# Recurrent mixer of a hybrid encoder: level products of both directions in one group, projection banks emptied by ScalarE ahead of the sigmoids, outputs in the places of the level tiles

## The chip, the core and the metric

The kernel runs on one core of one Trainium2 chip. Its engines have names in the profile: PE is TensorE (PEld its weight loads), DVE VectorE, ACT ScalarE, POOL GpSimd, SP SyncE, which issues most of the DMAs. The metric is the device time of one execution in microseconds (us), as the median of several runs; one further execution is taken by the profiler, and all busy times, waits and windows come from that one.

## What is computed

The program is a two-layer encoder trunk on 1024 tokens of width 1024 in fp32. Layer 0 mixes tokens by windowed attention, layer 1 by a bidirectional gated linear recurrence (HGRN2); in both, four more heads attend to 256 memory tokens (the cross heads), and a ConvGLU channel mixer follows. Only layer 1's recurrence is touched. It has 8 heads of 128 keys and 128 values. Cut to what matters:

```python
q, i, zf, zb, gate, xq = split(u @ w_in, ...)        # 8 heads x 128 each, xq for the cross heads
q = silu(q); v = i
f = lb + (1 - lb) * sigmoid(z)                        # z = zf forward, zb backward
log_f, k = log(f), 1 - f
# per direction, over time:  S_t = diag(f_t) S_(t-1) + k_t v_t^T ;  o_t = q_t S_t
o = gla(q, k_f, v, log_f_f) + flip(gla(flip(q), flip(k_b), flip(v), flip(log_f_b)))
o = rmsnorm(o, norm_g) * silu(gate)                   # per head
y = concat([o, cross_attention(xq, mem_kv)]) @ w_out
```

## The kernel before

Every fp32 product against a weight is done as three products of rounded halves: `mm3` (L79 to L82) writes high by high, high by low, low by high into one PSUM bank. A weight unit of 128 x 1024 is loaded, rounded by ACT (L75) and its remainder taken by DVE (L76). The normed input of the layer stands transposed in SBUF as `uh`, `ul`.

**Layer 1's mixer** is `hgrn()`. Per head `proj(h)` makes the projections: `proj_fm` the query `q` and the two forget inputs `s` (f and b), each in two halves of 512 tokens with channels on partitions, and `proj_tm` the value `V` and gate `G` for two heads at once with tokens on partitions. All of them fill banks with the tag `pj`, of which there are two. Forget banks are emptied by one Exp on ACT. Query and gate banks go through `sigmoid` (L1100 to L1102: Exp, Ln, Exp on ACT, written to SBUF) and then a DVE product that reads the bank once more (L1124, L1138), so a bank is held until that product. `ORD` is a table of text that sets the order of loads and projections per head; projections of head h+1 are written in the program behind head h. Odd heads have six banks to project (q, f, b in two halves), even heads besides these the values and gates of two heads. The last head's row leaves two of its projections ("later") between its directions.

**A head** (`head`) calls `direction` four times, in the order (forward, first half), (backward, second half), (forward, second half), (backward, first half); I call them A, B, C, D, or first to fourth. A direction goes over 512 tokens in four chunks of 128:

- ACT makes log f (`Ln` at L1188, tile `a_`) and k (L1186, L1187, L1189); DVE scans (L1191) within blocks of 16; ACT takes exponentials `EP`, `ER` (L1198, L1199) and two more (L1211, L1212).
- DVE and POOL form the operands of three levels (blocks of 16, 32 and 64, L1213 to L1235). A step of each level multiplies the decays of neighbouring blocks together. The operand tiles are `E1`, `E2`, `G32` and `G`.
- PE forms the level products into the bank `pa` of the direction (`block`, L1217 to L1219), each on a strip of 32 columns of the array (`tile_position`): 8 products of 64 columns, 16 of 32 for the blocks of 16, 8 of 32 for the next level.
- DVE picks the valid entries into `Az` (L1258), ACT or POOL adds the directions into `As` (L1262, L1264).
- PE transposes `ER` (L1267) into a bank `pt`, ACT copies it to `kT` (L1270), PE multiplies by v into `pu` (L1273), and DVE updates the states `S` (L1280).

Then `output` runs for the second and the first half: PE sums `As` by v and the decayed queries by `S` into `po` (L1295), ACT takes squares (L99), POOL the power (L92), DVE scales (`on`, L1302), PE transposes (L1306), ACT writes `ot` (L1325) and SP stores it. For the last head `ot` isn't stored; it becomes operand of the output projection. Between directions and outputs, `cross` puts units of the cross heads (`cross_unit`, L198 to L240), as `HX` says: in even heads one after C and one after D. A unit ends with ACT's copy to `xo` (L238) and its DMA. In the stretch of the last head the output projection's first pass (bank `pb`) starts.

**What sets the order.** The engines' instruction order is fixed when the program is built. A planner takes the program as written, runs a time model of its own, and lets instructions of later parts go ahead where their tiles are to be had; `high_priority(AHEAD)` lets a few go first, `issue_after` holds some behind another. A tile with a tag takes one of a fixed number of places, and these are handed out in the order in which the program asks for them: a tile gets its place when the tile that held it has had its last reader. On each engine the instructions then run strictly in the built order. Before, the tag `E` has 5 places and a direction asks for 7 of them (`a_`, `R`, `B`, `E1`, `E2`, `G32`, `G`); `q` has 3 places, `s` 5; `ot` and `xo` share one place of their own; `kT`, `on`, and the pairs for x and p one each.

Of the kernel before, what the change touches and what calls it, by code (L numbers as in the profile page):

```python
# [8 lines left out]
F32 = mybir.dt.float32  # L9
# [9 lines left out]
P = 128  # L19
# [27 lines left out]
def build(tc, A, out):  # L47
# [149 lines left out]
    def cross_unit(l, h, b, head, wp, tags, w0, pair, dead=False):  # L197
# [39 lines left out]
        ot = p[:, :2, :].rearrange("p a b -> p (a b)") if dead else w0.tile([P, 512], F32, tag=tags.get("xo", "xo"), bufs=1, name="xo")  # L237
# [802 lines left out]
    def hgrn():  # L1040
# [18 lines left out]
        tags = {"pj": ("pj", 2, psj), "ps": ("pt", 2, Bank), "pt": ("pt", 2, Bank), "po": [lambda x=x: bank(x, (P, 512)) for x in ("po", "pu")], "sm": 1, "xo": "ot"}  # L1059
# [11 lines left out]
        for d in range(2):  # L1071
            gf = early.tile([P, 512], F32, tag="E", bufs=5, name="gf")
            nc.sync.dma_start(gf, A["gmask"][d])
            dve.tensor_copy(gm[d], gf)
# [23 lines left out]
        def sigmoid(o, z):  # L1098

            act.activation(o, z, AF.Exp, scale=-1.0)  # L1100
            act.activation(o, o, AF.Ln, bias=1.0)
            act.activation(o, o, AF.Exp, scale=-1.0)  # L1102

        def proj_tm(h, us, ts):
# [3 lines left out]
            for t in ts[::2]:  # L1108
# [10 lines left out]
                for x in range(2):  # L1119
                    g = G[:, two, t + x, :]  # L1120
                    with tc.high_priority(AHEAD):
                        dve.tensor_copy(V[:, two, t + x, :], ps[x][:, :, 0, :])
                        sigmoid(g, ps[x][:, :, 1, :])
                        dve.tensor_tensor(g, ps[x][:, :, 1, :], g, op=ALU.mult)  # L1124

        def proj_fm(h, r, us, bws):
            for b, w in bws:
# [6 lines left out]
                if w == 0:  # L1134
                    q = eq.tile([P, 512], F32, tag="q", bufs=3, name="q")
                    with tc.high_priority(AHEAD):
                        sigmoid(q, ps)
                        dve.tensor_tensor(q, ps, q, op=ALU.mult)  # L1138
# [32 lines left out]
        def direction(h, r, d, b, qin, S, As):  # L1171
# [5 lines left out]
            def E():  # L1177
                return early.tile([P, 512], F32, tag="E", bufs=5, name="E")
# [9 lines left out]
            act.activation(a_, k, AF.Ln, bias=lb[:, d, h:h + 1], scale=oml[:, d, h:h + 1])  # L1188
            act.activation(k, k, AF.Identity, bias=oml[:, d, h:h + 1], scale=noml[:, d, h:h + 1])  # L1189
            R, B = E(), E()  # L1190
            dve.tensor_tensor_scan(B[:, rev], smask, a_[:, rev], 0.0, op0=ALU.mult, op1=ALU.add)  # L1191
# [8 lines left out]
            pa = PA[d]  # L1200
            E1, E2 = E(), E()
            Bl, Be = halves(B, 16)
            Rl, Re = halves(R, 16)
# [7 lines left out]
            act.activation(e1, Re, AF.Exp, scale=-1.0)  # L1211
            act.activation(l2, Bl, AF.Exp, scale=-1.0)  # L1212
# [4 lines left out]
            def block(c, i, j, x, y, n=32):  # L1217

                return pe.matmul(pa[i:i + 32, c, j:j + n], x[:, c * P + i:c * P + i + 32], y[:, c * P + j:c * P + j + n],  # L1219
                                 start=True, stop=True, tile_position=(0, i))  # L1220

# [36 lines left out]
            dve.copy_predicated(Az[d], gm[d], pa.rearrange("p c t -> p (c t)"))  # L1258
            a2 = lambda x: x.rearrange("p c t -> p (c t)")
# [322 lines left out]
```

## Time and profile before

| | |
|---|---|
| median of 3 runs | 2642.74 us (2639.37 to 2643.58) |
| the profiled execution | 2641.9 us, span 2640.1 us |
| mean granted TensorE clock | 0.997 |
| busy in the span | PE 98%, DVE 67%, ACT 53%, POOL 18% |
| recurrent mixer, 1212 to 1890 us | PE 667.86 of 678 us, DVE 478.83, ACT 381.11, POOL 175.52, granted clock 1.00, DMA share 0.32 |

Rows of the profile read so: a group has its line, engine, operation and tiles (out<-in), the count behind x, then busy us and mean ns of one, then the idle time of the engine just before and what ended it. A row of the timeline begins with start and duration in us. A matmul's recorded duration includes its way through the array: back to back, products of 512 columns start closer together than their durations say. A wait row names engine, tile and line that waited, what released it, and total us, times, longest us.

### The profile page before, as it was taken

What the parts mean: (1) busy time and instruction counts of PE and PEld (TensorE: products, weight loads), DVE (VectorE), ACT (ScalarE), POOL (GpSimd) and SP (SyncE); (2) the same over time, 40 slices, a digit from 0 to 9 for tenths busy, and PEclk for the clock granted to TensorE, in tenths of its full rate; (3) what the DMA queues carried; (4) which work ended last, traced back from release to release, by engine and by line L of the source; (5) the groups of instructions that cost most, each with busy time, mean ns of one, the idle gap of its engine ahead of it and who ended that gap; (6) DMA issues with size and microseconds to landing.
All of it is one profiled execution on the core that took longest, in us unless ns stands there. A gap on an engine that the chain in (4) does not pass through costs nothing.

```text
span 2640.1 us, 38891 instructions
## 1 busy us (share of the span) xinstructions
PE 2595.8 (98%) x14372; PEld 2180.1 (83%) x14372; DVE 1757.6 (67%) x2852; ACT 1400.3 (53%) x2534; POOL 470.5 (18%) x520
## 2 busy tenths in 40 slices
PE   8999999999999999999999999999999999999998
PEld 8988888888888888887888878888887788888887
DVE  6778777587565565487577685767657665656457
ACT  6667767445444445455465564646434444444443
POOL 0421110221111100032134131221211111110013
PEclk9999999999999999999999999999999999999999
DMA  9782232467877756773236351113337777775666
GB/s 356 248 190 47 74 114 61 131 185 187 215 195 202 196 160 222 220 265 123 84 114 158 94 119 41 61 48 97 120 112 198 197 193 199 205 203 168 201 210 235
DMA packets 195727, 425.92 MB, mean 161 GB/s; under 512 B 20049, under 2 KB 56273, under 8 KB 189905
## 3 DMA queue, kind: packets, MB, share of 16 engines
q1 hardware_dynamic: 161552, 324.06, 37.9%
q0 software_dynamic: 24544, 90.19, 16.3%
q10 hardware_dynamic: 9440, 9.19, 1.0%
q8 instruction: 113, 1.85, 0.3%
q14 instruction: 78, 0.63, 0.1%
HBM read 330.04 MB, written 116.39 MB: 169 GB/s over the span
## 4 chain that ended last, share of the span: by engine, by line
PE 83%; DVE 8%; DMA 4%; ACT 3%; issue 1%; POOL 1%; SPq 0%; ACTq 0%; DVEq 0%; POOLq 0%
PE X L584 28%; PE V L584 10%; PE pj L80 7%; PE pj L81 7%; PE pj L82 7%; PE Y L584 5%; PE pb L80 4%; PE pb L81 4%; PE pb L82 4%; PE po L1295 1%; PE pt L386 1%; PE pa L1219 1%; PE pu L1273 1%; DVE wl L86 1%; PE po L390 1%
## 5 line engine op out<-in xcount | busy, mean ns | idle before, releaser
L86 DVE TENSOR_TENSOR wl<-st,wh 128x1024 fp32r<-128x1024 f32 (+1 forms) x238 | 263.3, 1112 | 314.0 <-ACT wh L85 283.1
L85 ACT CAST wh<-st 128x1024 fp32r<-128x1024 f32 (+1 forms) x238 | 222.5, 936 | 278.3 <-PE X L584 173.8
L584 PE MATMUL X<-wl,wh 128*128 128x512 f32 x528 | 205.0, 390 | 0.2 <-DVE wl L86 0.2
L80 PE MATMUL pj<-uh,wh 128*128 128x512 f32 x512 | 203.5, 398 | 1.7 <-DVE q L1138 1.4
L584 PE MATMUL X<-wh,wl 128*128 128x512 f32 x528 | 204.9, 389 | 0.0
L81 PE MATMUL pj<-ul,wh 128*128 128x512 f32 x512 | 202.3, 395 | 0.0
L82 PE MATMUL pj<-uh,wl 128*128 128x512 f32 x512 | 201.8, 394 | 0.0
L584 PE MATMUL X<-wh 128*128 128x512 f32 x528 | 198.8, 390 | 0.1
L80 PE MATMUL pj<-wh,uh 128*128 128x384 f32 (+1 forms) x512 | 188.3, 369 | 2.1 <-DVE gs L1124 1.2
L81 PE MATMUL pj<-wl,uh 128*128 128x384 f32 (+1 forms) x512 | 187.1, 365 | 0.0
L82 PE MATMUL pj<-wh,ul 128*128 128x384 f32 (+1 forms) x512 | 187.0, 365 | 0.0
L584 PE MATMUL V<-uh,wl 128*128 128x512 f32 x336 | 130.7, 389 | 0.0
L584 PE MATMUL V<-ul,wh 128*128 128x512 f32 x336 | 130.7, 389 | 0.0
L584 PE MATMUL V<-uh,wh 128*128 128x512 f32 x336 | 130.7, 389 | 0.0
L76 DVE TENSOR_TENSOR wl<-st,wh 128x1024 fp32r<-128x1024 f32 (+1 forms) x90 | 114.3, 1274 | 24.3 <-ACT wh L75 22.6
L584 PEld LDWEIGHTS X<-wl,wh 128*128 128x128 f32 x528 | 99.1, 188 | 21.5 <-DVE wl L86 0.9
L584 PEld LDWEIGHTS X<-wh 128*128 128x128 f32 x528 | 99.0, 188 | 21.3 <-ACT wh L85 0.6
L584 PEld LDWEIGHTS X<-wh,wl 128*128 128x128 f32 x528 | 99.1, 188 | 20.6
L80 PEld LDWEIGHTS pj<-uh,wh 128*128 128x128 f32 x512 | 96.2, 188 | 20.5 <-DVE q L1138 2.0
L75 ACT CAST wh<-st 128x1024 fp32r<-128x1024 f32 (+1 forms) x96 | 96.6, 1013 | 29.9 <-PE pj L81 15.4
L82 PEld LDWEIGHTS pj<-uh,wl 128*128 128x128 f32 x512 | 96.3, 188 | 18.9
L81 PEld LDWEIGHTS pj<-ul,wh 128*128 128x128 f32 x512 | 96.4, 188 | 18.4 <-DVE ul L86 0.4
(410 smaller groups left out, 7117.7 us busy)
## 6 DMA issues: line engine op xcount, KB each, us to landing
st<-hid SPq DMA_DIRECT2D x154, 256.0 KB, 3.2
st<-in_ffw_dram SPq DMA_DIRECT2D x108, 256.0 KB, 3.3
w2s<-in_ffw_dram POOLq DMA_DIRECT2D x24, 1024.0 KB, 8.4
st<-in_ffw_dram SPq DMA_DIRECT2D x46, 512.0 KB, 4.5
hid<-tt SPq DMA_DIRECT2D x88, 256.0 KB, 4.7
st<-w2s SPq DMA_DIRECT2D x88, 256.0 KB, 3.1
sx<-in_ffw_dram SPq DMA_DIRECT2D x84, 256.0 KB, 3.9
sy<-in_ffw_dram SPq DMA_DIRECT2D x42, 512.0 KB, 6.2
```

What stands on the lines that cost most here:

```text
L75: act.copy(h[:, :n], raw)
L76: (eng or dve).tensor_tensor(l[:, :n], raw, h[:, :n].bitcast(F32), op=ALU.subtract)
L80: pe.matmul(o, ah, bh, start=first, stop=False)
L81: pe.matmul(o, ah, bl, start=False, stop=False)
L82: return pe.matmul(o, al, bh, start=False, stop=last)
L85: act.copy(h, src)
L86: dve.tensor_tensor(l, src, h.bitcast(F32), op=ALU.subtract)
L386: pe.transpose(tp[:, j, :], sm[:, j, c * P:(c + 1) * P], ident)
L390: pe.matmul(po, v[:, lo + c, :], pl, start=False, stop=c == hi - lo - 1)
L584: last = pe.matmul(o, x, y, start=first and i == 0, stop=i == len(ops) - 1, skip_group_check=not first)
L1219: return pe.matmul(pa[i:i + 32, c, j:j + n], x[:, c * P + i:c * P + i + 32], y[:, c * P + j:c * P + j + n], start=True, stop=True, tile_po ...
L1273: pe.matmul(pu[:, c, :], kT[:, c, :], r["v"][:, 4 * b + c, :], start=True, stop=True)
```

## The change

Three edits, all in `hgrn()` and in the line of `cross_unit` that places its output.

1. **Level products.** `direction` no longer issues them; it returns its operand tiles. A new function `scores` issues them for both directions after each pair (A, B) and (C, D): first the products of 64 columns, each held behind the last and the two directions taking turns (they use different pairs of strips), then the blocks of 16 of both, then those of 32. `Az` and `As` follow there. A direction now uses `E1` and `E2` in place of `a_`, `R` and `B`, so it asks for 4 places of E and not 7.
2. **Projection banks.** Query and gate banks are emptied by ACT: an Exp into a tile `e` (one place) and a copy of the raw values to SBUF. Ln, Exp and the DVE product then work in SBUF; for the gate both token halves of 256 are merged into 512.
3. **Places.** Ring E has 8 places instead of 5, and `xo` and `ot` now draw from it. `kT` shares the place of `on`; the cross pairs for x and p share one pair of places.

```diff
-        ot = ... w0.tile([P, 512], F32, tag=tags.get("xo", "xo"), bufs=1, name="xo")
+        ot = ... w0.tile([P, 512], F32, tag=tags.get("xo", ("xo", 1))[0], bufs=tags.get("xo", ("xo", 1))[1], name="xo")
...
-        tags = {..., "xo": "ot"}
+        tags = {..., "xo": ("E", 8)}
...
-        def sigmoid(o, z):
+        def sigmoid(o):
 
-            act.activation(o, z, AF.Exp, scale=-1.0)
             act.activation(o, o, AF.Ln, bias=1.0)
             act.activation(o, o, AF.Exp, scale=-1.0)
+
+        def etile():
+            return wp.tile([P, 512], F32, tag="e", bufs=1, name="e")
...
-                for x in range(2):
-                    g = G[:, two, t + x, :]
-                    with tc.high_priority(AHEAD):
+                e = etile()
+                e4 = e.rearrange("p (h x c) -> p h x c", h=2, x=2)
+                g = G[:, two, t:t + 2, :]
+                with tc.high_priority(AHEAD):
+                    for x in range(2):
+                        act.activation(e4[:, :, x, :], ps[x][:, :, 1, :], AF.Exp, scale=-1.0)
                         dve.tensor_copy(V[:, two, t + x, :], ps[x][:, :, 0, :])
-                        sigmoid(g, ps[x][:, :, 1, :])
-                        dve.tensor_tensor(g, ps[x][:, :, 1, :], g, op=ALU.mult)
+                        act.copy(G[:, two, t + x, :], ps[x][:, :, 1, :])
+                    sigmoid(e)
+                    dve.tensor_tensor(g, g, e4, op=ALU.mult)
...
+                    e = etile()
                     with tc.high_priority(AHEAD):
-                        sigmoid(q, ps)
-                        dve.tensor_tensor(q, ps, q, op=ALU.mult)
+                        act.activation(e, ps, AF.Exp, scale=-1.0)
+                        act.copy(q, ps)
+                        sigmoid(e)
+                        dve.tensor_tensor(q, q, e, op=ALU.mult)
...
-                return early.tile([P, 512], F32, tag="E", bufs=5, name="E")
+                return early.tile([P, 512], F32, tag="E", bufs=8, name="E")
...
-            a_ = E()
+            E1, E2 = E(), E()
...
-            R, B = E(), E()
+            R, B = E1, E2
...
-            act.activation(e1, Re, AF.Exp, scale=-1.0)
-            act.activation(l2, Bl, AF.Exp, scale=-1.0)
+            act.activation(e1, e1, AF.Exp, scale=-1.0)
+            act.activation(l2, l2, AF.Exp, scale=-1.0)
...
-            with tc.high_priority(AHEAD):
-                for c in range(4):
-                    for o in (0, 32):
-                        mm = block(c, er * 64 + o, lt * 64, G, G, 64)
-                with tc.issue_after(mm.ins):
-                    for c in range(4):
-                        for o in range(0, P, 32):
-                            block(c, o, o, E2, E1)
-                    for c in range(4):
-                        for o in (0, 64):
-                            block(c, o + er * 32, o + lt * 32, G32, G32)
...
-            kT = wp.tile([P, 4, P], F32, tag="kT", bufs=1, name="kT")
+            kT = wp.tile([P, 4, P], F32, tag="on", bufs=1, name="kT")
...
+            return E1, E2, G32, G
+
+        def scores(ops, bs, As):
+
+            def block(d, c, i, j, x, y, n=32):
+                return pe.matmul(PA[d][i:i + 32, c, j:j + n], x[:, c * P + i:c * P + i + 32], y[:, c * P + j:c * P + j + n],
+                                 start=True, stop=True, tile_position=(0, i))
+
+            with tc.high_priority(AHEAD):
+                mm = None
+                for c in range(4):
+                    for d in (1, 0):
+                        G = ops[d][3]
+                        for o in (0, 32):
+                            with tc.issue_after(mm.ins) if mm else nullcontext():
+                                mm = block(d, c, d * 64 + o, (1 - d) * 64, G, G, 64)
+                with tc.issue_after(mm.ins):
+                    for d in (1, 0):
+                        for c in range(4):
+                            for o in (0, 32, 64, 96):
+                                block(d, c, o, o, ops[d][1], ops[d][0])
+                    for c in range(4):
+                        for d in (1, 0):
+                            for o in (0, 64):
+                                block(d, c, o + d * 32, o + (1 - d) * 32, ops[d][2], ops[d][2])
+            a2 = lambda x: x.rearrange("p c t -> p (c t)")
+            for d in (0, 1):
+                b = bs[d]
+                dve.copy_predicated(Az[d], gm[d], a2(PA[d]))
...
-            ot = wp.tile([P, 512], F32, tag="ot", bufs=1, name="ot").rearrange("p (c t) -> p c t", c=4)
+            ot = early.tile([P, 512], F32, tag="E", bufs=8, name="ot").rearrange("p (c t) -> p c t", c=4)
...
-                return [wp.tile([P, 512], F32R, tag=kind + c, bufs=1, name=kind + c) for c in "hl"]
+                return [wp.tile([P, 512], F32R, tag="x" + c, bufs=1, name=kind + c) for c in "hl"]
...
-                direction(h, r, d, b, qin[d], S[d], As)
+                ops[d] = direction(h, r, d, b, qin[d], S[d])
+                if i % 2:
+                    scores(ops, (b, 1 - b) if d == 0 else (1 - b, b), As)
```

Lines behind these edits have other numbers in the changed kernel: the Ln of log f is L1197 there, the ER transposes L1249, the state products L1255, the level products L1269, `Az` L1292, the output products L1311, the `on` transposes L1322 and `ot` L1341.

How the built order moves shows at three places. The first is ACT between heads 4 and 5 before the change: head 5's first direction (L1186 to L1212) amid cross work of head 4 (`ph`), ahead of head 4's `ot`, which comes further down.

```order
L85 CAST ph<-pt 128x512
L1143 ACTIVATE s<-pj 128x512
L1186 ACTIVATE s<-s 128x512
L1187 ACTIVATE s<-s 128x512
L1188 ACTIVATE E<-s,lb,oml 128x512
L1189 ACTIVATE s<-s,oml,noml 128x512
L85 CAST ph<-pt 128x512
L1270 COPY kT<-pt 128x384
L1198 ACTIVATE EP<-E 128x512
```

The same place of ACT after the change, with `xo`, both `ot` of head 4, and then head 5's Ln:

```order
L238 COPY xo<-pu 128x512
L1341 ACTIVATE ot<-pt,bng 128x512
L99 ACTIVATE junk,oss<-po 128x128
L239 DMA oT_58<-xo 128x512
L193 CAST kvh<-kvl 128x512
L1341 ACTIVATE ot<-pt,bng 128x512
L1197 ACTIVATE E<-s,lb,oml 128x512
L1198 ACTIVATE s<-s,oml,noml 128x512
L1207 ACTIVATE EP<-E 128x512
L1208 ACTIVATE ER<-E 128x512
```

Head 5's Ln has moved from ahead of head 4's last `ot` to right behind it; the same holds for every head from 1 to 7.

The second place is PE at the same point after the change: the end of head 4's last output (`po`), a cross unit's last products (`pu<-ph,kvh`), the transposes of `on`, and head 5's first ER transposes.

```order
L1311 MATMUL po<-S,qin 128x128 x2
L80 MATMUL pu<-ph,kvh 128x512
L81 MATMUL pu<-pl,kvh 128x512
L82 MATMUL pu<-ph,kvl 128x512
L1322 MATMUL pt<-ident,on 128x128 x4
L1249 MATMUL pt<-ident,ER 128x128 x4
L80 MATMUL pj<-uh,wh 128x512
L81 MATMUL pj<-ul,wh 128x512
```

Before, head 5's first ER transposes (L1267) stood amid projection products; now nothing stands between them and the transposes of `on`. In front of head 3 it is the same, in front of head 1 there are 38 products between, in front of head 7 there are 11, and in front of heads 2, 4 and 6 there are 63 to 76.

The third place is PE in the last head after the change, from the last `pb` product of the output projection ahead of it (11 such stand behind head 6's `on` transposes) to its last direction.

```order
L82 MATMUL pb<-wh,ul 128x512
L1249 MATMUL pt<-ident,ER 128x128 x4
L1255 MATMUL pu<-v,kT 128x128 x4
L1269 MATMUL pa<-E 32x64 x16
L1269 MATMUL pa<-E 32x32 x48
L1249 MATMUL pt<-ident,ER 128x128 x4
L1255 MATMUL pu<-v,kT 128x128 x4
L1249 MATMUL pt<-ident,ER 128x128 x3
L1255 MATMUL pu<-v,kT 128x128 x3
L1269 MATMUL pa<-E 32x64 x16
L1269 MATMUL pa<-E 32x32 x48
L1249 MATMUL pt<-ident,ER 128x128 x3
```

Before, the four directions of head 7 had `pb` products between them; now the four follow one another, and the `pb` products stand ahead of them and behind the outputs.

More of the change, by code (lines that the diff above doesn't have):

```diff
@@ L1169, in proj, with direction @@
             return r
-        def direction(h, r, d, b, qin, S, As):
+        def direction(h, r, d, b, qin, S):
             q, k = r["q"][b], r["s"][d][b]
@@ L1339, in cross @@
                     xhead[0] = cross_head(1, xh_, wp)
-                cross_unit(1, xh_, xb_, xhead[0], wp, tags, wp, pair, not units)
+                cross_unit(1, xh_, xb_, xhead[0], wp, tags, early, pair, not units)
         def head(h, r):
```

31 lines of the change are left out of this document (11 added, 20 removed).

## The prediction

> **What bounds the kernel now.** I read the page's busy shares first, then the stretch table for the mixer's eight heads, then TensorE's waits in it.
>
> ```profile
> PE 2595.8 (98%) x14372; PEld 2180.1 (83%) x14372; DVE 1757.6 (67%) x2852; ACT 1400.3 (53%) x2534; POOL 470.5 (18%) x520
> 1237.00:1868.00 631.00, 622.53 (x5022) 523.27 (x5020) 445.83 (x885) 352.04 (x756) 166.13 (x178) 1.00 0.31 89
> PE pt L1267 <- ACT ot L1325: 2.6, 2, 1.4
> PE pt L1306 <- DVE on L1302: 2.1, 3, 1.2
> PE pu L1273 <- DVE S L1280: 1.8, 2, 1.4
> PE pj L80 <- DVE q L1138: 1.4, 1, 1.4
> PE pj L80 <- DVE gs L1124: 1.2, 1, 1.2
> ```
>
> The second row runs from the first to the last group of level products: 631.00 us, then busy time of PE, PEld, DVE, ACT, POOL, the granted clock, DMA. PE works 622.5 of 631 at full clock; ACT's 352 and DVE's 446 are cover. The waits (total, times, longest) are all the mixer loses. So only PE counts: a change pays in PE's work or those few waits, and costs where it makes PE wait. PE keeps its order, so what stands ahead of a waiting instruction is all that hides the wait.
>
> **Level products: -16.** One direction's group in before:
>
> ```profile
> 1237.43 0.39 PE L80 MATMUL pj<-uh,wh 128*128 128x512 f32 x1
> 1237.66 0.39 PE L81 MATMUL pj<-ul,wh 128*128 128x512 f32 x1
> 1237.98 1.17 PE L1219 MATMUL pa<-E 128*32 128x64 f32 x64
> 1239.08 0.50 PE L82 MATMUL pj<-uh,wl 128*128 128x512 f32 x1
> 1239.41 0.39 PE L80 MATMUL pj<-wh,uh 128*128 128x512 f32 x1
> ...
> L1219 PE MATMUL pa<-E 128*32 128x32 f32 x1536 | 27.2, 199 | 0.0
> ```
>
> From L81's start to the last row's are 1.75 us with two 512-column products, whose starts are 0.23 apart (first two rows): the group costs 1.75 - 0.46 = 1.29, and 32 cost 41.3. It has 8 products of 64 columns on two of four strips, 16 of 32 on all, 8 of 32 on two. If strips run side by side, the fullest has 8 + 4 + 4 = 16 units of 32 columns, 1.17 / 16 each. A pair now does 64-column products on four strips (8 units), 8 for the level of 16, 4 for that of 32: 20 instead of 32. 1.17 x 20 / 16 = 1.46, plus 0.12 of edges, is 1.58; 16 pairs cost 25.3. Bounds: -1.9 if strips don't overlap and only 16 edges go, -20.6 if a pair costs one old group.
>
> **Banks, copies, multiplications: -6.**
>
> ```profile
> L1270 ACT COPY kT<-pt 128x512 f32<-128x512 f32 x16 | 9.4, 585 | 4.4 <-PE pt L1267 4.4
> L1100 ACT ACTIVATE gs<-pj 128x256 f32<-128x256 f32 x32 | 12.3, 384 | 64.8 <-DVE v L1122 64.6
> L1101 ACT ACTIVATE gs<-gs 128x256 f32<-128x256 f32 x32 | 13.4, 419 | 0.8
> L1101 ACT ACTIVATE q<-q 128x512 f32<-128x512 f32 x16 | 10.1, 632 | 0.4
> ```
>
> Banks now come free after one Exp and one copy on ACT, not after three activations and a DVE product: the 1.4 + 1.2 above go. Of the other 6.5 I take half, since their places in the order change; -6 in all, bounds -2.6 and -9.1. ACT gains 16 copies of 512 (0.59) and 32 of 256 (0.38, the second row), 21.6 us, and merging two 256-wide sigmoids into one of 512 saves 3.3 in each of two functions (last two rows), 6.6. These 15 us lie under PE's 631, price 0; uncovered, 15. DVE's merged products are off the path too.
>
> **Shared places: +74.** Ring E gives its places in program order. In before it is the level tiles' own:
>
> ```profile
> 1643.09 0.82 ACT L1188 ACTIVATE E<-s,lb,oml 128x512 f32<-128x512 f32 x1
> 1678.18 0.66 PE L1306 MATMUL pt<-ident,on 128*128 128x128 f32 x4
> 1684.21 0.69 ACT L1325 ACTIVATE ot<-pt,bng 128x512 f32<-128x512 f32 x1 [1.25 <-DMA oT<-ot]
> ```
>
> Head 5's first Ln runs 41 us ahead of head 4's last `ot`. Now `ot` and `xo` draw from the ring, and the order shows every head's first Ln on ACT behind the previous head's last `ot`, thus behind the `on` transposes on PE. What PE has between those transposes and the first ER transposes is the cover. By the order: 63 to 76 projection products in even heads (14 us and more, enough), 38 for head 1, none for heads 3 and 5, 11 for head 7. What is uncovered is this chain, shown by before's last direction:
>
> ```profile
> 1851.62 0.81 ACT L1188 ACTIVATE E<-s,lb,oml 128x512 f32<-128x512 f32 x1
> 1857.63 1.22 DVE L1191 TENSOR_TENSOR_SCAN E<-smask,E 128x512 f32<-128x512 bf16 x1
> 1859.56 0.73 DVE L1258 COPY_PREDICATED Az<-gm,pa 128x512 f32<-128x512 uint8 x1
> 1860.52 1.52 DVE L1214 TENSOR_TENSOR E<-ER,s 128x256 f32<-128x256 f32 x1
> 1862.96 0.34 DVE L1280 SCALAR_TENSOR_TENSOR S<-S,dec,pu 128x128 f32<-128x128 f32 x1
> 1866.77 0.42 DVE L1227 TENSOR_TENSOR EP<-EP 128x256 f32<-128x256 f32 x1
> 1867.11 0.55 DVE L1257 TENSOR_TENSOR ER<-ER,s 128x384 f32<-128x384 f32 x1
> ```
>
> Scan to ER is 1867.66 - 1857.63 = 10.0; without the foreign Az (0.65) and three S (0.8) it is 8.6, and the G that the group waits for is there 1.0 to 1.3 sooner, 7.5 after the scan. For a head's first direction: `ot` 0.7, Ln 0.8, chain 8.6, hand-overs 0.3 = **10.4** after the transposes. For the second, whose DVE work lies behind the first's, PE has 6.8 ahead of its group, 0.8 short. The third's tiles take the places that the first group frees, so its ER comes some 12.7 after that group starts (1.6 + Ln 0.8 + 8.6, and S and Az pieces of 1.7); in odd heads PE has 8.3 there (24 projection products, group, transposes, state products): 4.4 short. In before the third direction didn't wait for that.
>
> The remaining rows are for head 7 and head 5's outputs:
>
> ```profile
> 1883.93 2.46 PE po L1295 x22
> 1889.44 1.13 DVE L1302 SCALAR_TENSOR_TENSOR on<-po,ors,gs 128x128 f32<-128x128 f32 x4 [0.15 <-POOL ors L92]
> 1851.84 1.05 PE L1273 MATMUL pu<-v,kT 128*128 128x128 f32 x8
> 1852.73 0.60 PE L1267 MATMUL pt<-ident,ER 128*128 128x128 f32 x4
> 1869.03 1.29 POOL L1264 TENSOR_TENSOR As<-As,Az 128x512 f32<-128x512 f32 x1
> L76 DVE TENSOR_TENSOR wl<-st,wh 128x1024 fp32r<-128x1024 f32 x51 | 66.9, 1313 | 8.4 <-ACT wh L75 6.6 <-PE pt L1306 0.6
> ```
>
> From `po`'s end (1886.39) to `on`'s end (1890.57) are 4.2; before head 5 only three products (0.7) stand in it: 3.5.
>
> - Head 1: 10.4 - 38 x 0.23 = 1.8 (rounded), then 0.8 and 4.4: 7.0.
> - Head 3: 10.4 + 0.8 + 4.4 = 15.6.
> - Head 5: 3.5 + 10.4 + 0.8 + 4.4 = 19.1.
> - Head 7, where the order leaves no projection between its four directions. First: 10.4, two weight splits on DVE (1.2 each), less 11 products (2.5), about 10. Second: 7.5 less PE's 1.3 (the rows at 1851.84 and 1852.73: 4 transposes 0.44, 4 state products 0.9) = 6.2. Third: 12.7 less PE's 3.1 (group 1.6, then 1.5 as for the second) = 9.6. Fourth, whose scan stands ahead of the third's ER: 8.6 - 1.3, less 1.3 since the group needs G only, less 1.0 on PE = 5.0. Last As on POOL, 1.2 uncovered. 32.0.
>
> Together 73.7. Bounds: the chain has one product of 1.52 (L1214), its neighbours take 0.4; at that it is 7.5, 1.1 less in eight waits, -9. Upward, directions that DVE runs beside other work are spaced so:
>
> ```profile
> 1548.43 1.37 DVE L1191 TENSOR_TENSOR_SCAN E<-smask,E 128x512 f32<-128x512 bf16 x1 [0.84 <-PE pa L1219]
> 1559.74 1.22 DVE L1191 TENSOR_TENSOR_SCAN E<-smask,E 128x512 f32<-128x512 bf16 x1
> 1572.15 2.04 DVE L1191 TENSOR_TENSOR_SCAN E<-smask,E 128x512 f32<-128x512 bf16 x1 [0.41 <-PE pa L1219]
> ```
>
> 11 to 12 us apart is 3 more in each of 13 waits, +39. I take 8.6: PE's waits leave DVE little else. `kT` and the x and p pairs share places at a cost that lies in these waits: 0.
>
> **Clock: +14.** A wait costs more than itself:
>
> ```profile
> 2049.45 0.79 PE L584 MATMUL X<-u7h,wh 128*128 128x512 f32 x1 [4.32 <-ACT u7h L85]
> 2049.00:2055.00 6.00, 5.55 (x13) 4.39 (x14) 4.71 (x5) 2.75 (x4) 0.86 (x1) 0.50 0.28 56
> 2055.00:2059.00 4.00, 4.00 (x19) 3.26 (x19) 2.96 (x4) 2.72 (x5) 0.00 (x0) 1.00 0.31 92
> ```
>
> After 4.32 us idle the clock stood at 0.50 for 5.5 us of work, then 1.00: 2.7 lost. Five of the waits outside head 7 reach 4 us: 13.5. Head 7 has little PE work between waits, so little to slow: 0.5. Bounds 0 and 27. The Trainium skill (TensorE: Matmul & The Clock Gate, Part 1: The HAM clock gate) has the clock halve after an idle window of about 3.4 us and return after about as much steady work; by it a wait loses 1.7 or more, an estimate of 17 over ten waits. The 5.5 us here are longer than its 3.4; the trace's own figure goes into the sum.
>
> **Sum:** -16 - 6 + 74 + 14 = +66. On the profiled execution's 2641.9 that is 2707.9; the median of the runs shown is 0.8 above that execution, so **2709**.
>
> **Rivals.**
> - *Only head 7 pays.* If PE arrives late enough at heads 1, 3 and 5 that other work covers their chains, 32, some 2 of outputs and 4 of clock stay, less 22: 2641.9 + 16, about 2658. For it: even heads are covered so. Against: in heads 3 and 5 the order has nothing between.
> - *Strips don't overlap.* The group then saves 1.9, not 16: 2709 + 14 = 2723. For it: one product of 32 columns takes 199 ns, and nothing in before has different products on all strips for long. Against: 64 records in 1.17.
> - *Faster.* The new waits are covered, as if ring E still let directions run ahead: 2641.9 - 22, about 2620. For it: before's waits are tiny with ACT idle 279 of 631. Against: PE and ACT would have to break their written order. It decides if the first `ot` to ER takes under 3 us.
> - *Same.* Head 7's waits, halved (16), with 4 of clock and 2 of outputs eat the 22: 2642. For it: only the tails of four heads are concerned. Against: heads 3 and 5 would have to be free of theirs.
>
> **How the numbers follow.** Forecast 0.62; its own range 2676 (2641.9 - 20.6 - 9.1 + 64, no clock loss) to 2748 (the wide spacing, the rest as taken). Only head 7 0.14; strips 0.10; faster 0.10; same 0.04. 0.2% (5.3 us) is what a measurement here tells from no change. The range 2652 to 2748 takes in the first three. Faster 0.10, same 0.04, slower 0.86.
>
> **What would show it.** Right: PE waits of about 10 us ahead of the `pt` transposes of ER in heads 3 and 5, four waits of 4 to 10 in head 7, clock 0.5 behind each, PE busy in the stage unchanged or less; a pair's group at 1.6. Wrong: heads 3 and 5 without such waits, or a pair's group near 2.5.

## The result

The changed kernel takes 2736.46 us (median of 4 runs, 2732.11 to 2738.23), the kernel before 2641.81 us in the runs beside it: a ratio of 1.0358, 95% interval 1.0345 to 1.0371. That is 94.6 us slower. The forecast was 2709, 66 us slower, in a range of 2652 to 2748: the direction held and the waits came where they had been named, but the size was a third too small.

The stretch table of the changed kernel, from the end of the first FFN to the start of the second, which holds the whole mixer (us, then busy time of PE, PEld, DVE, ACT, POOL, the granted clock, DMA):

```profile
1200.00:2084.60 884.60, 792.71 (x5777) 657.34 (x5776) 537.29 (x1043) 436.91 (x920) 205.11 (x216) 0.95 0.30 87
```

and the same stretch of the kernel before:

```profile
1198.00:1990.00 792.00, 781.18 (x5777) 653.86 (x5776) 548.00 (x1061) 426.87 (x905) 196.59 (x216) 1.00 0.33 98
```

The stretch grew by 92.6 of the 96.0 by which the span grew (2640.1 to 2736.1). PE is idle for 91.9 us of it (884.6 less 792.7), where it was for 10.8; it is also busy 11.5 longer, though the level products became cheaper. TensorE's waits there:

```profile
PE pt L1249 <- DVE ER L1246: 55.0, 9, 11.6
PE pa L1269 <- POOL E L1234: 8.6, 3, 4.5
PE pj L80 <- ACT q L1145: 6.8, 6, 1.9
PE pu L1255 <- ACT kT L1252: 5.8, 4, 3.0
PE pt L1322 <- DVE on L1318: 4.7, 1, 4.7
PE pj L80 <- DVE xl L86: 3.9, 4, 2.3
PE pj L80 <- ACT s L1152: 2.2, 4, 1.1
```

Nine waits for `ER` make 55 us; before, the whole list came to some 10. This is how the longest looks, in front of head 5, in the timeline of PE (the last `pu` product of a cross unit, the `on` transposes of head 4, the ER transposes of head 5 and the first projections behind them):

```profile
1730.39 0.40 PE L82 MATMUL pu<-ph,kvl 128*128 128x512 f32 x1
1735.47 1.16 PE L1322 MATMUL pt<-ident,on 128*128 128x128 f32 x4 [4.69 <-DVE on L1318]
1747.16 1.09 PE L1249 MATMUL pt<-ident,ER 128*128 128x128 f32 x4 [10.53 <-DVE ER L1246]
...
1748.47 0.63 PE L81 MATMUL pj<-ul,wh 128*128 128x512 f32 x1
1748.90 0.63 PE L82 MATMUL pj<-uh,wl 128*128 128x512 f32 x1
```

and in that of ACT and DVE:

```profile
1736.67 0.69 ACT L1341 ACTIVATE ot<-pt,bng 128x512 f32<-128x512 f32 x1 [2.33 <-PE pt L1322]
1737.25 0.80 ACT L1197 ACTIVATE E<-s,lb,oml 128x512 f32<-128x512 f32 x1
...
1738.09 1.23 DVE L1200 TENSOR_TENSOR_SCAN E<-smask,E 128x512 f32<-128x512 bf16 x1 [1.99 <-ACT E L1197]
...
1746.33 0.69 DVE L1246 TENSOR_TENSOR ER<-ER,s 128x512 f32<-128x512 f32 x1
```

`ot`, Ln, scan, eight microseconds of DVE, ER: the chain that the prediction summed to 10.4 us; measured 10.53, and 11.64 in front of head 3. The longest waits of the other odd heads, in the order of heads 1, 3, 3, 7 and 7:

```profile
1400.84 0.87 PE L1249 MATMUL pt<-ident,ER 128*128 128x128 f32 x3 [6.86 <-DVE ER L1246]
1558.59 1.08 PE L1249 MATMUL pt<-ident,ER 128*128 128x128 f32 x4 [11.64 <-DVE ER L1246]
1580.01 0.87 PE L1249 MATMUL pt<-ident,ER 128*128 128x128 f32 x3 [4.44 <-DVE ER L1246]
1938.96 1.11 PE L1249 MATMUL pt<-ident,ER 128*128 128x128 f32 x4 [10.92 <-DVE ER L1246]
1961.77 0.87 PE L1249 MATMUL pt<-ident,ER 128*128 128x128 f32 x3 [5.75 <-DVE ER L1246]
```

Behind the wait in front of head 5 PE starts at half pace (the last two rows of PE's timeline above start 0.43 apart, not 0.23).

### The profile page after: what moved, and what is told of

The parts are those of the page before. It is cut to its first block, busy times and chain, and to the rows that moved or that the text cites. A ratio compares the mean times of both kernels' runs of the same rounds, so it can differ in the third digit from the quotient of the medians.

```text
span 2736.1 us, 38844 instructions
## 1 busy us (share of the span) xinstructions
PE 2607.6 (95%) x14372; PEld 2182.4 (80%) x14372; DVE 1747.2 (64%) x2836; ACT 1410.9 (52%) x2550; POOL 479.6 (18%) x520
## 4 chain that ended last, share of the span: by engine, by line
PE 83%; DVE 8%; ACT 3%; DMA 3%; issue 2%; POOL 1%; ACTq 0%; SPq 0%; DVEq 0%; POOLq 0%
PE X L584 27%; PE V L584 10%; PE pj L80 7%; PE pj L81 7%; PE pj L82 7%; PE Y L584 5%; PE pb L80 4%; PE pb L82 4%; PE pb L81 4%; PE po L1311 1%; PE pt L386 1%; DVE wl L86 1%; DMA st<-hid 1%; DVE ER L1226 1%; PE pa L1269 1%
## 5 line engine op out<-in xcount | busy, mean ns | idle before, releaser
L1234 POOL TENSOR_TENSOR E<-EP,q 128x256 f32<-128x256 f32 x64 | 60.1, 940 | 386.9 <-DVE EP L1227 289.7
L75 ACT CAST wh<-st 128x1024 fp32r<-128x1024 f32 (+1 forms) x96 | 96.4, 1012 | 57.7 <-PE pj L81 44.7
```

Source lines behind the costliest of these rows:

```text
L75: act.copy(h[:, :n], raw)
L1234: pool.tensor_tensor(gl, pl_, ql, op=ALU.mult)
```

## The experiments

Twelve kernels ran in three groups, each beside the kernel before (medians of 2640.37, 2638.85 and 2639.91 us in the three groups). "Stretch" below is always the one from FFN to FFN, 792.0 us before and 884.6 after, of the profiled execution; waits are its length less PE's busy time.

### The outputs out of the ring

The changed kernel, with `xo` in the first 512 columns of its own `xp` tile (the first half; "second" in the expectation is a slip) and `ot` in the place of `on`:

```diff
-        tags = {..., "xo": ("E", 8)}
+        tags = {..., "xo": ("ot", 1)}
-            ot = early.tile([P, 512], F32, tag="E", bufs=8, name="ot")
+            ot = wp.tile([P, 512], F32, tag="on", bufs=1, name="ot")
-                cross_unit(1, xh_, xb_, xhead[0], wp, tags, early, pair, not units)
+                cross_unit(1, xh_, xb_, xhead[0], wp, tags, wp, pair, True)
```

> The changed kernel with its two outputs out of ring E: xo in the second half of its own xp tile's place (the first 512 columns, read last by the transposes), ot in the place of on. Nothing else is altered: grouped level products, emptied banks, 8 places of E for level tiles alone. The built order lets a head's first direction run ahead of the previous head's outputs again, as before the change. Theory (the shared ring costs the time): the 75 us of waits ahead of ER and pa in heads 1, 3, 5 and 7 go, with the clock loss behind them; 2615 to 2640, likeliest 2625. Rival (grouping makes the third direction and the first wait, wherever the outputs lie): waits of 4 to 10 us ahead of ER stay, 2700 or more. Rival (banks emptied by ScalarE are late): some 13 us of waits on pj banks stay and the rest goes, about 2640.

Measured: 2638.50 us, ratio to before 0.9997 (0.9987 to 1.0007): the whole loss is gone. Its stretch:

```profile
1203.50:1991.70 788.20, 771.62 (x5779) 646.54 (x5778) 540.20 (x1045) 436.46 (x921) 198.52 (x216) 1.00 0.33 98
```

and the longest of its waits:

```profile
PE pj L80 <- ACT q L1145: 5.1, 5, 3.1
```

Waits 16.6 (91.9 with the outputs in the ring), the granted clock 1.00 against 0.95, PE busy 771.6: 9.6 less than before, which is what grouping the level products saves here, and 21.1 less than in the changed kernel, which does the same products. So the place of the two outputs costs 75.3 of waits and 21.1 of slower products, 96.4 in all. Grouping and emptied banks together are worth some 4 in the stretch and nothing that the medians resolve. The time expected as likeliest, 2625, was missed by 13: PE's work fell by no more than 9.6, and its waits rose from 10.8 to 16.6. The rival by which grouping makes the waits falls. Of the rival with the late banks (13 us of bank waits, about 2640) the 5.1 above are left; the late banks can't be the cause of the loss.

### The ring alone

The kernel before, with `ot` and `xo` in ring E and nothing else:

```diff
-        ot = ... bufs=1, name="xo")
+        ot = ... bufs=6 if "xo" in tags else 1, name="xo")
...
-        tags = {..., "xo": "ot"}
+        tags = {..., "xo": "E"}
...
-                return early.tile([P, 512], F32, tag="E", bufs=5, name="E")
+                return early.tile([P, 512], F32, tag="E", bufs=6, name="E")
...
-            ot = wp.tile([P, 512], F32, tag="ot", bufs=1, name="ot")
+            ot = early.tile([P, 512], F32, tag="E", bufs=6, name="ot")
...
-                cross_unit(1, xh_, xb_, xhead[0], wp, tags, wp, pair, not units)
+                cross_unit(1, xh_, xb_, xhead[0], wp, tags, early, pair, not units)
```

> The kernel before with one thing of the change alone: ot and xo take their places in ring E, which has 6 places (its 5 and the one that ot and xo had). Level products by direction, banks and kT as before. The built order puts every head's first Ln behind the previous head's last output, as in the changed kernel. Theory (the shared ring): waits of 3 to 9 us ahead of the level products in odd heads and three of 8 in head 7, some 65 in all, and 10 of clock: about 2715, at least 2680. Rival (grouping, or the banks): neither is in it, 2640 to 2650.

Measured: 2706.43 us, ratio 1.0254 (1.0237 to 1.0271). Stretch and main waits:

```profile
1197.00:2054.00 857.00, 803.38 (x5781) 669.99 (x5780) 543.81 (x1060) 428.31 (x905) 201.97 (x216) 0.97 0.31 90
```

```profile
PE pa L1219 <- POOL E L1234: 20.8, 8, 5.9
PE pu L1273 <- ACT kT L1270: 8.9, 6, 2.5
PE pj L80 <- ACT s L1143: 6.7, 5, 2.1
PE pj L80 <- DVE gs L1124: 6.1, 2, 3.1
```

The sharing is enough to lose 66 us with level products, banks and `kT` as they were. Together with the first run this shows the cause from both sides: taken out of the change, the sharing takes the whole loss with it; put alone into the kernel before, it brings 66 of the 95 us. The waits (53.6) are fewer than the 65 expected and spread over more lines; PE's busy time rose by 22.2, double the 10 expected.

### The banks alone

The kernel before with the Exp into `e` and the copies by ScalarE of the change (the query's part is shown, the gate's is as in the change), and `kT` in the place of `on` to make room.

```diff
-                        sigmoid(q, ps)
-                        dve.tensor_tensor(q, ps, q, op=ALU.mult)
+                        act.activation(e, ps, AF.Exp, scale=-1.0)
+                        act.copy(q, ps)
+                        sigmoid(e)
+                        dve.tensor_tensor(q, q, e, op=ALU.mult)
-            kT = wp.tile([P, 4, P], F32, tag="kT", bufs=1, name="kT")
+            kT = wp.tile([P, 4, P], F32, tag="on", bufs=1, name="kT")
```

> The kernel before with the emptied banks alone (Exp into e and a copy by ScalarE, sigmoid in SBUF); kT goes into the place of on to make room for e. Theory as predicted: the bank waits go, 6 us less, about 2636. Rival (the banks' Exp and copy stand behind waiting work on ScalarE and are late, which the 13 us of pj waits in the changed kernel suggest): 5 to 10 us more, about 2650.

Measured: 2640.01 us, ratio 1.0001 (0.9992 to 1.0011). No difference. The longest of the waits of PE that are left:

```profile
PE pu L1282 <- DVE S L1289: 4.3, 4, 2.4
```

The two bank waits of before (L1138, L1124, 2.6 together) are indeed gone, and the wait for `S` went from 1.8 to 4.3: a wait moved. Neither the 6 us of gain nor the loss came.

### The change with the old banks, and with a ninth place

The changed kernel with `sigmoid` straight from the bank as before; then the same with ring E at 9 places (the room of `e`). The first undoes the second edit of the change as a whole, of which the query's part is shown; the second adds the last two lines.

```diff
-                        act.activation(e, ps, AF.Exp, scale=-1.0)
-                        act.copy(q, ps)
-                        sigmoid(e)
-                        dve.tensor_tensor(q, q, e, op=ALU.mult)
+                        sigmoid(q, ps)
+                        dve.tensor_tensor(q, ps, q, op=ALU.mult)
...
-                return early.tile([P, 512], F32, tag="E", bufs=8, name="E")
+                return early.tile([P, 512], F32, tag="E", bufs=9, name="E")
```

> The changed kernel with the banks as before (sigmoid straight from the bank, no e). The order is serial by head as in the changed kernel, but more projection products stand between a head's last on transposes and the next head's first ER: 49, 34, 48 and 61 in front of heads 1, 3, 5 and 7, where the changed kernel has 38, 14 (ahead of the second on transposes' successor none), none and 11. Theory (a wait is the 10.4 us chain less the products that stand in it): the first-direction waits of heads 3, 5 and 7 shrink from 11 each to 0 to 3, those of the third direction stay, 38 us of waits and 8 of clock, less 16 of grouping: about 2672. Rival (the serial order costs the same whatever stands in it, or the banks have nothing to do with it): 2725 to 2740.

> The changed kernel with the banks as before, and the place that e leaves given to ring E: 9 places instead of 8, still with xo and ot in it. If places are too few, a ninth lets the next head's tiles in earlier: 2690 or less, against 2723 with 8. If it is the order in which places are handed out, and not their number, nothing changes: 2710 to 2730.

Measured: 2723.21 us, ratio 1.0316 (1.0298 to 1.0333), and with nine places 2713.59, ratio 1.0277 (1.0262 to 1.0292). The first expectation, 2672, missed by 51 us. Waits of the first:

```profile
PE pt L1240 <- DVE ER L1237: 26.1, 7, 7.0
PE pj L80 <- ACT s L1143: 8.8, 6, 3.3
PE pj L80 <- DVE q L1138: 5.9, 5, 2.1
...
PE pj L80 <- DVE gs L1124: 4.8, 3, 2.2
```

The waits for `ER` did halve, 55.0 to 26.1, as counting the products ahead of them said. But the projections, which stand there now, wait themselves (s, q, gs: 19.5 where the changed kernel has 9.0 for q and s). Cover moved to one wait was missing at another. The ninth place brings 10 us of the 83 that this kernel loses to the one before. So one place more undoes little of the loss. More than nine were not tried: that the order of handing out binds, and not the number of places, is argued from this and not shown.

### One output at a time

The changed kernel with only `xo` out of the ring (into `xp`), and with only `ot` out of it (into the place of `on`). The first two lines are the one, the last two the other:

```diff
-                cross_unit(1, xh_, xb_, xhead[0], wp, tags, early, pair, not units)
+                cross_unit(1, xh_, xb_, xhead[0], wp, tags, wp, pair, True)
...
-            ot = early.tile([P, 512], F32, tag="E", bufs=8, name="ot")
+            ot = wp.tile([P, 512], F32, tag="on", bufs=1, name="ot")
```

> The changed kernel with xo alone out of ring E (into the place of its own xp tile); ot stays in the ring. The order stays serial by head, but 66, 57, 57 and 63 projection products now stand ahead of the first ER of heads 1, 3, 5 and 7 (38, none, none and 11 in the changed kernel), 40 to 48 ahead of the third's. Theory by counting cover (a wait is its chain less the products ahead of it): only head 7 waits, some 12 us, 4 of clock, less 12 of level products: about 2645. Theory by the chain (a head's directions and outputs now follow one another, an odd head takes 73 us on DVE and ScalarE from its first Ln to the next head's where it took 61, and products put ahead of one wait are missing at another, as in the run with the old banks): 12 in each odd head, 10 to 15 in head 7 and clock: about 2690. Rival (xo is the cause): 2640 or less.

> The changed kernel with ot alone out of ring E (into the place of on); xo stays in the ring. A head's first direction may pass the outputs, but in odd heads not the xo behind the fourth direction of the even head; 38 products stand ahead of it. Counting cover: 1.8 ahead of the first and 4.4 ahead of the third direction in heads 1, 3 and 5, about 20 of waits and 8 of clock, less 12: about 2655. If ot is all of the cause: 2640 or less; if xo alone is: 2700 or more.

Measured: with `ot` alone in the ring 2666.02 us, ratio 1.0100 (1.0085 to 1.0115); with `xo` alone 2691.89, ratio 1.0195 (1.0180 to 1.0210). Both cost, `xo` twice as much; 27 and 53 us over before, against 95 for both. Both came out above what counting cover gave (2645, 2655), the first below the chain's 2690. With `xo` alone the waits are not where I counted them:

```profile
PE pj L80 <- ACT s L1152: 13.5, 10, 3.3
PE pt L1249 <- DVE ER L1246: 11.9, 4, 3.9
PE pj L80 <- DVE xl L86: 9.2, 4, 2.3
```

The third directions wait 11 us as counted (three of 3.6 to 3.9), and 23 more fall on projections and on the split of a cross unit's bank, which the count had left out.

### Filling the waits

The changed kernel with products that nobody needs in five of the longest waits:

```diff
             tp = bank("pt")
+            for _ in range({(3, 0, 0): 44, (5, 0, 0): 44, (3, 0, 1): 16, (5, 0, 1): 16, (1, 0, 1): 24}.get((h, d, b), 0)):
+                pe.matmul(tp.rearrange("p c t -> p (c t)"), uh[:, 0, :P], uh[:, 0, :512], start=True, stop=True)
```

> The changed kernel with products that nobody needs put ahead of the ER transposes where it waits longest: 44 (10 us) before the first direction of heads 3 and 5, 16 (3.7 us) before their third, 24 (5.5 us) before the third of head 1, all into the bank that the transposes then overwrite. They take no longer than the waits that they stand in. If a wait also costs by the clock that it leaves behind (2.7 us each, as predicted): 10 to 15 us less than the changed kernel, about 2723, and the granted clock near 1.00 behind those waits. If the waits cost only themselves: 2736, as the changed kernel.

Measured: 2737.01 us, ratio 1.0364 (1.0346 to 1.0381), the changed kernel's 1.0358. The fillers did what they should, in front of head 5:

```profile
1731.34 10.31 PE L1249 MATMUL pt<-uh 128*128 128x512 f32 x44 [0.84 <-ACT ot L1343]
1742.08 0.66 PE L1251 MATMUL pt<-ident,ER 128*128 128x128 f32 x4 [0.42 <-DVE ER L1246]
1742.70 0.50 PE L80 MATMUL pj<-uh,wh 128*128 128x512 f32 x1
1743.04 0.39 PE L81 MATMUL pj<-ul,wh 128*128 128x512 f32 x1
1743.27 0.39 PE L82 MATMUL pj<-uh,wl 128*128 128x512 f32 x1
```

The wait is filled, and the projections behind start at the full pace of 0.23. Yet the medians show no gain. One of its waits tells where some of the faster products went:

```profile
PE pj L80 <- ACT q L1145: 13.1, 10, 2.2
```

In the changed kernel that was 6.8 in 6 waits. PE comes sooner to the next bank and waits there for ScalarE. But the stretch, cut at the first ER transposes of head 7, shows more (the changed kernel's two parts, then this one's):

```profile
1200.00:1938.96 738.96, 667.02 (x4947) 553.21 (x4946) 445.67 (x879) 380.19 (x799) 169.55 (x177) 0.96 0.29 84
1938.96:2084.60 145.64, 125.69 (x830) 104.14 (x831) 91.62 (x165) 56.72 (x121) 35.56 (x40) 0.90 0.31 105
1202.00:1934.40 732.40, 692.13 (x5093) 573.15 (x5092) 446.83 (x879) 381.51 (x800) 167.36 (x177) 0.99 0.29 85
1934.40:2083.00 148.60, 128.79 (x829) 107.01 (x830) 92.30 (x165) 56.82 (x121) 35.47 (x40) 0.86 0.31 103
```

The part with the fillers is 6.6 shorter, at a better clock; the part behind, where nothing was filled, is 3.0 longer at a worse one. The planner also built another order on ScalarE: `kT`'s copy near 1402.69 in the changed kernel stands ahead of one to `q`, and behind it with the fillers (1404.95, 1402.73). So the stretch is 3.6 shorter, where 10 to 15 had been expected, and the interval of the ratio, some 5 us to either side, can't tell 3.6 from nothing. This run doesn't show that the slow products behind a wait cost no time.

### The scan twice

In the kernel before and in the changed one, the line of the scan (L1191, L1200) stands twice, the second writing the same values (of the changed kernel):

```diff
             dve.tensor_tensor_scan(B[:, rev], smask, E1[:, rev], 0.0, op0=ALU.mult, op1=ALU.add)
+            dve.tensor_tensor_scan(B[:, rev], smask, E1[:, rev], 0.0, op0=ALU.mult, op1=ALU.add)
```

> The kernel before with the scan of each direction done twice (the second writes the same values): 32 x 1.36 = 43 us more on DVE, all in the chain of a direction. Theory (directions run far enough ahead in before that PE hides their chain): 0 to 5 us more. Rival (DVE's work counts in either kernel): 20 us or more.

> The changed kernel with the scan of each direction done twice, as in the run beside it. Theory of the chain (a head's four directions and its outputs follow one another, and in odd heads and head 7 nothing hides them): 1.36 for each direction of heads 1, 3, 5 and 7, 16 x 1.36 = 22, with some in the even heads: 15 to 35 us over the changed kernel, about 2760. Rival (PE sets the time and the waits are a few places in its order): 5 or less for the first directions of heads 3, 5 and 7, about 2741.

Measured: 2651.99 us, 12.1 over before (ratio 1.0041, 1.0028 to 1.0055), and 2775.75, 39.3 over the 2736.46 of the changed kernel, which ran in another group (ratios to before 1.0520, 1.0502 to 1.0538, against 1.0358). The stretch of the changed kernel with the scan twice:

```profile
1198.00:2120.70 922.70, 801.84 (x5779) 662.93 (x5778) 577.78 (x1076) 437.46 (x921) 197.63 (x216) 0.93 0.28 84
```

and of the kernel before with it:

```profile
1200.00:1999.80 799.80, 784.02 (x5779) 655.27 (x5778) 583.35 (x1092) 426.30 (x905) 202.09 (x216) 1.00 0.32 97
```

DVE works 40.5 us longer in the changed kernel (577.78 less 537.29) and its stretch grows by 38.1; in the kernel before 35.4 and 7.8. The 12.1 there lie between the 0 to 5 expected and the rival's 20: PE hides most of the chain before, not all of it. The 38 in the changed kernel are more than the upper end of what I had expected (35), and they mean that even heads pay too, although 63 to 76 products stand in front of them. From the last `on` transposes of an odd head to those of the next odd head, which is one even and one odd head, the changed kernel takes 186.0, 185.1 and 182.7 us (they start at 1438.11, 1624.09, 1809.21 and 1991.95) and with the scan twice 196.8, 194.9 and 194.3 (1441.90, 1638.73, 1833.60, 2027.92): 10 to 12 more, where eight scans are 10.1 (a quarter of 40.5). So in the changed kernel the chain of the directions is on the path in even and odd heads alike, and in the kernel before it is mostly covered. Of the 38.1, 29.0 are waits of PE and 9.1 longer busy time at a lower clock (0.93 against 0.95); that both together make nearly the length of the added scans fits a chain that sets the time, and doesn't prove it alone. The built order also moved a little.

### What is left of the change without the ring

The grouped level products with the old banks, ring E for level tiles alone, `xo` in `xp`; the room of `e` goes to `ot` in the one, to `kT` in the other (`ot` then takes the place of `on`). The second's lines that differ from the change, besides the old banks and `xo`:

```diff
-            kT = wp.tile([P, 4, P], F32, tag="on", bufs=1, name="kT")
+            kT = wp.tile([P, 4, P], F32, tag="kT", bufs=1, name="kT")
-            ot = early.tile([P, 512], F32, tag="E", bufs=8, name="ot")
+            ot = wp.tile([P, 512], F32, tag="on", bufs=1, name="ot")
```

> The grouped level products without the rest that hurts: banks as before (no e), ot in a place of its own again (the room of e), xo in its own xp tile's place, ring E for level tiles alone. The level products save 10 to 12 of PE's busy time; if the waits stay at before's 11 us, 2630; if they rise as in the run with ot in the place of on (17), 2637.

> As the run beside it, but the place that e leaves goes to kT, and ot takes the place of on: a head's next first direction then waits for no output place at all. If kT in the place of on was what cost the 6 us of waits in the first of these kernels, 2630 or less; if not, as that one, 2638.

Measured: 2647.48 us, ratio 1.0026 (1.0016 to 1.0036), for the first, worse than either expectation; 2635.19 us, ratio 0.9979 (0.9970 to 0.9988), for the second, which beats both kernels by a little. The stretch of the second:

```profile
1201.00:1985.00 784.00, 769.53 (x5780) 644.17 (x5779) 543.33 (x1060) 429.89 (x905) 195.31 (x216) 1.00 0.33 99
```

The second has PE busy 11.7 less than before and waits of 14.5 instead of 10.8. The two differ in two places at once, so which of them costs the 12 us stays open; the first waits 4.5 us for `kT` copies (three of 2.1 at most) that the second's list of waits doesn't have.

## Why the prediction was right, and where it was wrong

By its own steps, in the stretch from FFN to FFN (+92.6 of the profiled 96):

| step | predicted | measured | from |
|---|---|---|---|
| new waits at the places named | +74 | +75 | the changed kernel's trace, by head below |
| other waits | -6 | +6 | 91.9 - 74.7 = 17.2 left, 10.8 before |
| level products | -16 | -10 | PE busy, outputs out of the ring: 771.6, before 781.2 |
| clock | +14 | +21 | PE busy, changed kernel 792.7, outputs out of the ring 771.6 |
| sum | +66 | +92 | |

The measured column has to come to the growth of the stretch, since a stretch is PE's busy time and its waits; it says where the time shows on PE and not what makes it.

**Shared places** held, as the cause and in the size of the waits, head by head: predicted 7.0, 15.6, 19.1 and 32.0 for heads 1, 3, 5 and 7, measured 9.2, 16.1, 18.8 and 30.6. In head 1 most went to the third direction (6.86, with 1.08 and 1.25 ahead); in heads 3 and 5 the second direction's 0.8 did not come, and in head 7 the last As waited 0.2 and not 1.2. That the run without the sharing and the run with the sharing alone agree makes the cause shown, not argued. The price 0 for the places of `kT` and of the x and p pairs held too: the run with the outputs out of the ring keeps them and takes the time of before, as far as the medians tell.

**The single waits were right, the reason for the sum was not whole.** The step that failed is "what PE has between those transposes and the first ER transposes is the cover". Counting products ahead of one wait forecasts that wait, and did so again, if roughly, for `ER` with the old banks and with `xo` alone. But three times (old banks, each output alone) the time fell less than the count said, by 51, 21 and 37 us. Products moved in front of one wait are taken from another place: with the old banks the waits for `ER` fell by 28.9 and those of the projections rose by 10.5. And the doubled scan cost 38 of its 40.5 us in the changed kernel, in heads that the count called covered too. So what stands in front of a single wait is not what hides a head's chain; the chain's own length comes through.

**Banks, -6:** failed. The two bank waits go in the kernel before, but the time doesn't move (1.0001), since PE's waits in the stretch fall from 10.8 to 8.6 and its busy time rises from 781.18 to 783.43; and in the changed kernel PE waits for emptied banks 6.8 us (q) besides 3.9 for a cross unit's split. The price 0 for ScalarE's copies holds in the kernel before, where they are covered (its busy time rose by 8.3 there and by 10.0 in the changed kernel, where 15 were worked out). With the ring the emptied banks come with a built order that costs 13 us more than with the old banks (2723.21).

**Level products, -16:** the group of a pair came out nearly as worked out. In the changed kernel's timeline:

```profile
1253.10 0.39 PE L81 MATMUL pj<-wl,uh 128*128 128x512 f32 x1
1253.42 1.56 PE L1269 MATMUL pa<-E 128*32 128x64 f32 x128
1254.91 0.50 PE L80 MATMUL pj<-wh,uh 128*128 128x512 f32 x1
1255.25 0.40 PE L81 MATMUL pj<-wl,uh 128*128 128x512 f32 x1
```

From 1253.10 to 1255.25 are 2.15, less two products of 0.23: 1.69 for a pair, against 1.58 predicted and 2 x 1.29 before. So the strips do work side by side, and the rival in which they don't falls. 16 x 1.69 = 27 against 41.3 would be 14, and the 10 in the stretch understate it: the run with the outputs out of the ring has two stretches of 3.4 us at a granted clock of 0.50 (1531.6 to 1535.0 and 1849.1 to 1852.5), which lost 3.4. In the last of the kernels above, at 1.00 throughout, PE is busy 11.7 less than before. So the term was sized 2 to 4 us too high.

**Clock, +14:** PE's loss is real and larger. In the changed kernel 42.9 us of PE's work lie in nine stretches at a granted clock of 0.50, which loses 21.4; one of them stands behind a wait of 1.88 us and one behind 2.29, where I had counted waits from 4 us on. This term makes up +7 of the 26 us that were missed; the other waits make up 12, the level products 6 and the waits named 1. Whether it adds its whole size to the time stays open: filling five waits made the part with the fillers 6.6 us shorter, and the whole time no shorter that the runs can tell. One sign that was to show the prediction right did not come: PE's busy time was to stay unchanged or fall (-16 and +14 leave -2), and it rose by 11.5.

**Rivals:** "only head 7 pays" is out (heads 1, 3 and 5 wait 44 us). "Faster", with the waits covered, and "same" are out with it; the engines kept their written order. The strips are answered above.

What stays open: which engine's part of the chain weighs most (the doubled scan lengthens DVE's work and the chain at once), how much of the slower products is time, and why `ot` and `xo` cost 27 and 53 apart and 95 together.

## What to carry to other kernels

A ring of places that is handed out in program order is also a queue: a tile that is asked for late in one iteration and lies in the ring of the next iteration's first tiles puts the iterations one behind another, though there is room. Before sharing a place, compare in the built order which tile of the next round stood ahead of the newcomer. And where an engine starts to wait in many places, adding up the waits less their cover can fall short, as it did here; lengthen the suspected chain by a known amount, and see what share of it the time pays.

## What the runs showed of the hardware

The clock falls after shorter waits than I had bounded. I had taken waits of 4 us as those that cost; in the changed kernel a wait of 2.29 us was enough:

```profile
1321.80 0.50 PE L80 MATMUL pj<-uh,wh 128*128 128x512 f32 x1 [2.29 <-DVE xl L86]
1322.13 0.39 PE L81 MATMUL pj<-ul,wh 128*128 128x512 f32 x1
...
1323.21 0.63 PE L82 MATMUL pj<-uh,wl 128*128 128x512 f32 x1
1323.64 0.63 PE L80 MATMUL pj<-uh,wh 128*128 128x512 f32 x1
```

The first products still start 0.23 apart, and from one microsecond behind the restart on they start 0.43 apart, for eight products or 3.4 us (the next at full pace starts at 1326.20). The same came behind a wait of 1.88 us (restart at 1673.73) and not behind one of 1.38 (1658.20). The Trainium skill (TensorE: Matmul & The Clock Gate, Part 1: The HAM clock gate) asks for an idle window of about 3.4 us before the half clock; 2.29 us is less, so here the measurement decides. Its figure for the cold array, 426.7 ns from start to start for 512 columns (same part, Wait — 56ns, not 53.3ns?), agrees with the 0.43.
